# Four modulations move from TensorE's blocks in the attention stages to VectorE's sums in the feed-forward stages

## The chip, the cores and the metric

The kernel runs on one core of a Trainium2 chip. The metric is the device time of one execution in microseconds (us), as the median of several runs; before the change it is 1739.68 us (three runs, 1738.67 to 1740.33). A core has five engines with an instruction queue each: TensorE (PE, its weight loads shown apart as PEld), VectorE (DVE), ScalarE (ACT), GpSimd (POOL) and SyncE (SP, which here issues most DMAs).

## The reference

Two layers of a diffusion transformer's block over 256 tokens x and 256 context tokens, width 1024. A layer has a half feed-forward, an attention with three branches, and a second half feed-forward. Each of the three is normed, shifted, scaled and gated by modulations, nine a layer, each a product of a condition with a 1024 x 1024 piece of `w_ada`. There are two conditions (one for the tokens, one for the context).

```python
mod_x = (jax.nn.silu(c) @ w_ada[l] + b_ada[l]).reshape(bn, 1, N_MOD, d)
mod_c = (jax.nn.silu(c_ctx) @ w_ada[l] + b_ada[l]).reshape(1, 1, N_MOD, d)
h_x = _half_ffn(h_x, norm_g[l, 0], mod_x[:, :, 0], mod_x[:, :, 1], mod_x[:, :, 2], ffn1_up[l], ffn1_down[l])
a_x = _modulate(_rmsnorm(h_x, norm_g[l, 1]), mod_x[:, :, 3], mod_x[:, :, 4])
p_x = a_x @ w_in[l]
...
h_x = h_x + mod_x[:, :, 5] * (jnp.concatenate([o_a, o_b, o_c], axis=-1) @ w_out[l])
h_x = _half_ffn(h_x, norm_g[l, 2], mod_x[:, :, 6], mod_x[:, :, 7], mod_x[:, :, 8], ffn2_up[l], ffn2_down[l])
```

The context goes the same way, except that it ends with the second layer's attention. So modulations are numbered 0 to 17 over both layers (9 is the second layer's first); those from 14 on are needed for one condition only. The result is the normed h_x. All products are wanted in float32 precision.

## The kernel before

**Stages.** The program is one long sequence: feed-forward 1 of layer 0 (about 15 to 407 us of the trace), attention 0 (to about 612) with the w_out product behind it, feed-forward 2 of layer 0 (from about 640), feed-forward 1 of layer 1 (from about 1010), attention 1 (1377 to 1513) with its w_out product, feed-forward 2 of layer 1, and the final norm. Activations lie with features on partitions and tokens on the free axis; 512 tokens (both halves) go together where the context takes part, 256 where it does not.

**Dense products.** Each weight and each activation is kept as a high and a low part, and `mm3` (L344) makes three matmuls of one product: L348, L349 and L350. A stream of weight blocks is loaded by SP into three raw buffers of 1 MB (RAW_BUFS); `emit_split` (L291) makes from a piece of a block a slot of the pool `w`: ScalarE casts the high part (L306), VectorE subtracts for the low one (L309). The pool has 7 buffers (W_BUFS). `pump` splits ahead of need while the count of slots out, `st["out"]`, is below a limit `st["look"]` (6 in the feed-forward stages, less in the attentions); `take` (L331) hands out the next slot, and splits it on the spot if that was not done. `by_halves` (L532) is the start of a stage's products: it takes four slots and goes through one half of the tokens and then the other, as the normed operand comes from `apply` (ScalarE L437, VectorE L436 and L431), while the end of the stage before, `proj_out` (L466), still adds its last chunks to the residual (VectorE L461) and squares them (ScalarE L374).

**Modulations, two ways.** By TensorE: blocks of 128 rows by 2048 columns (two modulations, 1 MB) stand in the weight stream, between the attention's own blocks. `ada_quantum` (L175) multiplies one with four matmuls of 32 columns of weights and 512 moving columns (L181); eight blocks make a pair of modulations, which ScalarE copies out (L239) and TensorE turns into columns (L246). By VectorE: `ada_one` (L201) loads 128 rows by 512 columns (256 KB, L207) two blocks ahead and adds their multiple to an accumulator of the pool `w`, for each condition, with ScalarE for the first rows (L219) and VectorE for the others (L221). At the end of a modulation `ada_total` (L225) sums over the partitions with four matmuls against ones (L229), some time after the last block: 22 us by the emission clock, or 5 for an urgent one (2 or 8, where it is the first of its stage). Until then the accumulator counts as a slot out. Sixteen blocks make a modulation. `ada_step`, called once for each slot of a feed-forward stage, does ADA_RATE blocks, or 2 for an urgent modulation. Which modulation goes which way is set by MODS (by stage, VectorE) and ATT (by layer, pairs for TensorE).

**Order.** The order of each engine's instructions is that in which the Python code emits them. A clock of emitted TensorE work (`tick`) starts the deferred pieces (`later`). In an attention `run` (L928) goes through softmax units: scores (L838, L839) of one unit, work to fill in, then the transposes of the probabilities of the unit two before (`flip`: L878 for tokens, L883 for the context, copied out by ScalarE, L886). Products with v follow (`pv`: L912, its normalization's transposes L919, ScalarE L920 and L924). How many us of filling work stand in each gap is a table, FILL, and `piece` (L1048) picks it: the rest of w_in's products, products with v, the pooling (`pooled`: L1025, then ScalarE L1029 and VectorE L1030), then by turns a modulation block (`run_ada`) and two chunks' dense products with w_out's first half (`rest_out`, six matmuls for each chunk of two). What dense work is left after the last unit comes behind the last product with v.

Of the kernel before, what the change touches and what calls it, by code (L numbers as in the profile page):

```python
# [18 lines left out]
TX = 256  # L19
# [3 lines left out]
EPS = 1e-6  # L23
# [9 lines left out]
MODS = ((2, 3, 4, 5, 8), (9, 10, 11, 12), (13, 14, 15))  # L33
ATT = ([3], [8])
ADA_RATE = (1.3, 1.3, 1.3, 1)
# [15 lines left out]
def dit_kernel(  # L51
# [47 lines left out]
    pending = []  # L99
    clock = [0.0]  # L100
# [21 lines left out]
    stream = []  # L122
# [52 lines left out]
    def ada_quantum(g, k, raw):  # L175
        """128 rows of two of the modulations, by the tensor engine."""
        if k == 0:
            ada_ps[g] = ps_ada.tile([128, 512], F32, tag="ada", name="ada")
        ps = ada_ps[g]
        for j in range(4):  # L180
            PE.matmul(out=ps[32 * j:32 * j + 32, :], lhsT=sc[:, k, :], rhs=raw[:, j * 512:(j + 1) * 512], start=(k == 0), stop=(k == KD - 1))  # L181
        st["raws"] -= 1
        loads()
        if k == KD - 1:
            sb = ada_rows(ada_ps.pop(g))
            later(5.0, lambda: ada_columns(sb, [2 * g, 2 * g + 1], 2))
# [3 lines left out]
    def conds(m):  # L190
        """How many conditions a modulation is for: the context's tokens end with the second layer's attention."""
        return 1 if m >= 14 else 2
# [8 lines left out]
    def ada_one():  # L201
        """The next block of the modulations, 128 rows by 512 columns, that the vector engine does: it sums both conditions'
        multiples of the rows; the sums over partitions are the tensor engine's, once for a modulation."""
# [38 lines left out]
    def ada_columns(sb, ms, n):  # L242
        """Rows 32j (and the one after) of four groups of columns become columns of the modulations ms."""
# [27 lines left out]
    def next_main(force=False):  # L271
        """Whether the next weight block of the stream is on its way; ada blocks before it go to the tensor engine."""
# [7 lines left out]
    def run_ada():  # L280
        """Runs the next ada block of the stream, if that is what comes next."""
# [9 lines left out]
    def emit_split(between=None):  # L291
        """Splits the next slot of the stream into two float32r parts (ada blocks on the way go to the tensor engine)."""
# [51 lines left out]
    def mm3(ps, pairs, n, start, stop):  # L344
        """Accumulates products of split operands: pairs of ((wh, wl), (ah, al)); the first of each is stationary."""
# [17 lines left out]
    def acc_chunk(vs, k):  # L363
        """Squares of chunk k of the halves vs of the tokens; summed over chunks, but a half's last chunk apart."""
# [18 lines left out]
    def rsqrt(ps, n, scale):  # L383
        """1 / sqrt(ps * scale + EPS) of few elements, by Newton's steps from a guess at the exponent."""
# [27 lines left out]
    def spread(v, rb=None):  # L412
        """The tokens' factors on every partition."""
# [5 lines left out]
    def apply(v, i, a, pace=0.0, rb=None):  # L419
        """The operand of the next product: normed, scaled and shifted, in two parts."""  # L420
# [45 lines left out]
    def proj_out(src, kl, ppair, gate, both, final, after, each=None):  # L466
        """One part of a product into the residual. src(k) gives the moving operand; a slot has ppair chunks. In the final
        part the last two slots go by halves of the tokens, so that one half's norm runs under the other."""
# [35 lines left out]
    def boundary(i):  # L504
        """What follows a finished half: its statistic and its operand of the next product."""
# [26 lines left out]
    def by_halves(sl, a, both, evac):  # L532
        """Products of four slots, one half of the tokens after the other, chunk by chunk of the operand as it comes. Two
        products share a bank: the first start clears what the whole bank has had written."""
# [11 lines left out]
    def up_evac(pa, pb, g, m, nm, lo, hi):  # L546
        """g[m : m + nm] of the tokens lo:hi from the banks of both factors."""
# [89 lines left out]
    def attn_prep(l):  # L637
        """Bias of the neighbourhood's scores (masked), and the pooling weights as blocks of a diagonal."""
# [11 lines left out]
        # copies of a head's table at a pitch of 465, read back at a pitch of 464: row c starts c entries earlier  # L650
# [24 lines left out]
    def attention(l, a, both):  # L675
        """From the normed tokens to the operand of w_out and the first half of that product; both: the context's tokens
        are carried on too."""
# [20 lines left out]
        # k of the neighbourhood, k and v of the grouped heads: by halves of the tokens  # L698
        sl = [take() for _ in range(4)]

        def key_tile():
            """Keys of two heads: each one's high part on both halves of the rows, then both low parts; and some queries."""
# [12 lines left out]
        def split_queries(dst, src, scale=None):  # L715
            """Queries of two heads, each one's high part on its half of the rows and its low part on the other."""
# [10 lines left out]
        def rotate(q, n):  # L727
            """Rotary embedding of n chunks of the first TX tokens in place."""
# [15 lines left out]
        def k_post():  # L744
            """Norm and rotation of the grouped heads' keys."""
# [29 lines left out]
        # q and v of the neighbourhood  # L775
# [28 lines left out]
        # the pooling's matrices: each block of tokens on itself; on its neighbour they are in k_edge  # L804
# [9 lines left out]
        def queries(br, kind, hs):  # L814
            """Both heads' queries as they are multiplied."""
# [7 lines left out]
        def scores(br, kind, hs, t):  # L823
            """x: one block of 128 tokens over all keys; c: all of the context's tokens over its keys."""
# [42 lines left out]
        def flip(br, kind, hs, t, Ps):  # L867
            """Probabilities with the keys on partitions; the products with v once a pair of heads has them all."""
# [59 lines left out]
        def run(jobs, fill, before):  # L928
            """Units of softmax, each one's probabilities turned depth units later."""
# [19 lines left out]
        def stat_col(c, tb):  # L949
            """Where the statistics of chunk c's two heads lie, for a block of tokens."""  # L950
            return c // 2 * nb * 4 + tb * 4 + c % 2 * 2

        def q_post(j):
            """Rotation and norm of two chunks of queries."""
# [9 lines left out]
        def rest_in():  # L964
            """q of the grouped heads and u of the pooling."""
# [27 lines left out]
        def rest_out():  # L993
            """The product with w_out's first half: the neighbourhood's and the pooling's chunks."""
# [53 lines left out]
        def piece():  # L1048
            """A piece of the work that is independent of the units."""
# [21 lines left out]
        def before(n):  # L1071
            """What the unit n needs, beyond its queries."""
# [40 lines left out]
    with tc.manual_schedule():  # L1113
        # small operands, laid in rows and turned into columns
# [13 lines left out]
        def quarter_load(h, i, raw):  # L1128
            """Half of the rows of the first shift's and scale's chunks 2h and 2h + 1."""
# [19 lines left out]
        def load_pair(v, k2):  # L1149
            """Two chunks of half the tokens, turned."""  # L1150
# [7 lines left out]
        def quarter_ada(h):  # L1158
            """The products of two chunks of the shift and scale: each of the array's four groups of columns sums a quarter of
            the rows."""  # L1160
# [25 lines left out]
        # sums of squares of the tokens as they come, a token on a partition  # L1186
# [27 lines left out]
        def first():  # L1214
            """The first four slots' products, as the shift and scale and with them the operand's chunks come."""
# [45 lines left out]
        def last_chunk(ch):  # L1261
            """A chunk of the result, scaled by the last norm's gains."""
# [94 lines left out]
```

## Time and profile before

| | before |
|---|---|
| timed, median of 3 | 1739.68 us |
| profiled execution, span | 1741.7 us |
| dense products (L348, L349, L350), x7776 | 913.0 + 904.5 + 904.2 us of records that overlap |
| weight splits, casts L306 and subtractions L309, x312 each | 314.9 and 371.0 us |
| blocks of modulations by VectorE, L221, x308 | 216.0 us |
| blocks of modulations by TensorE, L181, 128 records (x64 matmuls) | 16.8 us by the sum of the groups of the instructions' table |
| totals L229, 96 records | 13.0 us |

The profiled execution's span lies 2.0 us above the timed median; sums are made against the span. A page row of an instruction group gives the line, the engine, the operation, what is written and read with the tile's partitions and elements, the count, the busy time, the mean length in ns, and the idle time of the engine just ahead with what ended most of it. A timeline row gives the start in us, the length, the engine, the line and the operation. Matmuls are pipelined, so the length of one is longer than the distance to the next; distances are taken from starts.

### The profile page before, as it was taken

Reading aid. Unit: us, or ns where it says so; the run is one execution under the profiler, and the core shown is the slowest. Engines: PE = TensorE matmul, PEld = TensorE weight load, DVE = VectorE, ACT = ScalarE, POOL = GpSimd, SP = SyncE. Lnnn points to the kernel's source line nnn. Section 1 sums busy time; section 2 is a strip of 40 time slices with the busy share of each in tenths; the row PEclk is TensorE's granted clock in tenths of the full one; section 3 lists DMA queues with packets and bytes.
Section 4 is the critical chain, followed back from the end, with each engine's and each line's share of the span. In section 5 each row is a group of like instructions: output and inputs, shape, how many; then the busy total and the mean of one; then the engine's idle time right before and its main releaser. Section 6 shows DMA issues by size and latency. Waiting matters only on the chain.

```text
span 1741.7 us, 23662 instructions
## 1 busy us (share of the span) xinstructions
PE 1706.1 (98%) x9512; PEld 1428.7 (82%) x9512; DVE 1025.0 (59%) x1748; ACT 664.8 (38%) x1087; POOL 33.3 (2%) x48
## 2 busy tenths in 40 slices
PE   6999999999999999999999999999999999989998
PEld 4778888889886688888888898888888987789998
DVE  5666676566545586666664466545433656565554
ACT  4431322324545644323333243223222356554443
POOL 0000200000000000000000000020000000000000
PEclk8999999999999999999999999999999999989999
DMA  9755555431304325544653335455533133546561
GB/s 316 207 175 168 155 179 173 151 121 49 109 25 160 107 73 168 164 140 140 192 152 122 92 88 183 150 160 174 146 97 97 49 110 146 169 133 205 164 201 50
DMA packets 295335, 246.48 MB, mean 142 GB/s; under 512 B 9377, under 2 KB 262442, under 8 KB 293176
## 3 DMA queue, kind: packets, MB, share of 16 engines
q1 hardware_dynamic: 292680, 241.30, 44.7%
q0 software_dynamic: 1088, 2.15, 0.5%
q8 instruction: 75, 1.23, 0.3%
q10 hardware_dynamic: 1456, 1.52, 0.3%
q14 instruction: 36, 0.29, 0.1%
HBM read 243.88 MB, written 2.00 MB: 141 GB/s over the span
## 4 chain that ended last, share of the span: by engine, by line
PE 90%; DVE 4%; DMA 2%; ACT 2%; issue 1%; SPq 0%; DVEq 0%; ACTq 0%
PE mm L348 27%; PE mm L350 27%; PE mm L349 27%; PE mm L839 2%; PE mm L912 1%; PE aux L878 1%; PE mm L838 1%; DVE w L309 1%; PE ada L181 1%; DMA ada_raw<-in_w_ada_dram 1%; DVE ada_acc L221 1%; PE ada L229 1%; DMA raw<-in_w_ada_dram 1%; ACT w L306 1%; PE aux L409 0%
## 5 line engine op out<-in xcount | busy, mean ns | idle before, releaser
L348 PE MATMUL mm<-act,w 128*128 128x512 f32 (+1 forms) x2592 | 913.0, 352 | 5.6 <-ACT act L437 3.3
L350 PE MATMUL mm<-act,w 128*128 128x512 f32 (+1 forms) x2592 | 904.2, 349 | 1.8 <-DVE w L309 1.8
L349 PE MATMUL mm<-act,w 128*128 128x512 f32 (+1 forms) x2592 | 904.5, 349 | 1.0 <-DVE act L431 0.9
L348 PEld LDWEIGHTS mm<-act,w 128*128 128x128 f32 x2592 | 494.1, 191 | 89.3 <-issue 19.4
L350 PEld LDWEIGHTS mm<-act,w 128*128 128x128 f32 x2592 | 494.0, 191 | 64.1 <-DVE w L309 2.4
L349 PEld LDWEIGHTS mm<-act,w 128*128 128x128 f32 x2592 | 494.3, 191 | 62.5 <-DVE act L431 1.7
L309 DVE TENSOR_TENSOR w<-raw,w 128x1024 fp32r<-128x1024 f32 (+1 forms) x312 | 371.0, 1198 | 245.6 <-ACT w L306 245.2
L306 ACT CAST w<-raw 128x1024 fp32r<-128x1024 f32 (+1 forms) x312 | 314.9, 1023 | 120.4 <-PE mm L350 93.6
L221 DVE SCALAR_TENSOR_TENSOR ada_acc<-ada_raw,sc,ada_acc 128x512 f32<-128x512 f32 x308 | 216.0, 746 | 47.9 <-DMA ada_raw<-in_w_ada_dram 24.7
L558 ACT CAST act<-gf 128x512 fp32r<-128x512 f32 (+1 forms) x87 | 49.7, 571 | 318.7 <-DVE gf L555 318.7
L461 DVE SCALAR_TENSOR_TENSOR hT<-mm,hgt,hT 128x256 f32<-128x256 f32 x168 | 75.1, 480 | 97.8 <-PE mm L350 97.6
L552 ACT ACTIVATE sil<-mm 128x512 f32<-128x512 f32 (+1 forms) x87 | 47.6, 547 | 214.8 <-PE mm L350 214.5
L555 DVE TENSOR_TENSOR gf<-sil,mm 128x512 f32<-128x512 f32 (+1 forms) x87 | 54.3, 625 | 94.0 <-PE mm L350 77.7
L559 DVE TENSOR_TENSOR act<-gf,act 128x512 fp32r<-128x512 f32 (+1 forms) x87 | 54.9, 631 | 55.5 <-ACT act L558 55.5
L374 ACT ACTIVATE sq<-hT 128x256 f32<-128x256 f32 (+1 forms) x52 | 25.5, 492 | 108.4 <-DVE hT L461 108.4
L437 ACT ACTIVATE act<-nt,modT 128x256 fp32r<-128x256 f32 x88 | 43.4, 507 | 49.3 <-DVE nt L436 49.2
L219 ACT ACTIVATE ada_acc<-ada_raw,sc 128x512 f32<-128x512 f32 x44 | 29.6, 718 | 47.4 <-DMA ada_raw<-in_w_ada_dram 36.7
L855 DVE TENSOR_REDUCE nm<-mm 128x1 f32<-128x512 f32 (+1 forms) x60 | 41.0, 686 | 7.9 <-PE mm L839 7.2
L863 ACT ACTIVATE P<-mm,nm,rq 128x512 f32<-128x512 f32 (+1 forms) x48 | 33.7, 707 | 22.3 <-DVE nm L860 21.0
L431 DVE SCALAR_TENSOR_TENSOR act<-nt,modT,act 128x256 fp32r<-128x256 f32 x88 | 41.3, 480 | 1.3 <-ACT act L437 1.3
L436 DVE SCALAR_TENSOR_TENSOR nt<-hT,gsc,aux 128x256 f32<-128x256 f32 x88 | 40.8, 476 | 1.8 <-PE aux L416 1.2
L886 ACT COPY PT<-aux 128x512 f32<-128x512 f32 x60 | 32.2, 588 | 16.9 <-PE aux L878 12.9
(154 smaller groups left out, 885.5 us busy)
## 6 DMA issues: line engine op xcount, KB each, us to landing
raw<-in_ffn_up_dram SPq DMA_DIRECT2D x172, 512.0 KB
ada_raw<-in_w_ada_dram SPq DMA_DIRECT2D x192, 256.0 KB
raw<-in_ffn_down_dram SPq DMA_DIRECT2D x32, 1024.0 KB
raw<-in_w_ada_dram SPq DMA_DIRECT2D x16, 1024.0 KB
raw<-in_ffn_down_dram SPq DMA_DIRECT2D x16, 768.0 KB
raw<-in_w_in_dram SPq DMA_DIRECT2D x10, 1024.0 KB
raw<-in_w_out_dram SPq DMA_DIRECT2D x8, 1024.0 KB
raw<-in_w_ada_dram SPq DMA_DIRECT2D x12, 512.0 KB
```

What stands on the lines that cost most here:

```text
L221: DVE.scalar_tensor_tensor(out=o, in0=raw, scalar=col, in1=o, op0=ALU.mult, op1=ALU.add)
L306: ACT.copy(out=wh, in_=sl)
L309: DVE.tensor_tensor(out=wl, in0=sl, in1=wh.bitcast(F32), op=ALU.subtract)
L348: PE.matmul(out=ps, lhsT=wh, rhs=ah, start=start and i == 0, stop=False)
L349: PE.matmul(out=ps, lhsT=wh, rhs=al, start=False, stop=False)
L350: PE.matmul(out=ps, lhsT=wl, rhs=ah, start=False, stop=stop and i == last)
L437: ACT.activation(out=acol(a, k, v * TX, v * TX + TX)[0], in_=t, func=AF.Identity, bias=modT[:, l * 72 + 3 * n * 8 + k, v:v + 1])
L461: DVE.scalar_tensor_tensor(out=hT[:, k, cols], in0=ps, scalar=gate[:, k, v:v + 1], in1=hT[:, k, cols], op0=ALU.mult, op1=ALU.add)
L552: ACT.activation(out=s[:, 0:n], in_=pa[:, 0:n], func=AF.Silu)
L555: DVE.tensor_tensor(out=u[:, 0:n], in0=s[:, 0:n], in1=pb[:, 0:n], op=ALU.mult)
L558: ACT.copy(out=gh, in_=uv)
L559: DVE.tensor_tensor(out=gl, in0=uv, in1=gh.bitcast(F32), op=ALU.subtract)
```

## The change

Three tables of numbers change; the rest of the diff deletes comments and docstrings. The pairs of modulations 6, 7 (`ATT` group 3) and 16, 17 (group 8) leave the weight stream, and join MODS: 6 and 7 in the first stage, 16 and 17 in the third. Modulation 8 moves from the first stage to the second. The rates of the first and third stage go from 1.3 to 1.5 blocks per slot. Blocks by stage were 80, 64 and 48; they are 96, 80 and 80.

```diff
-MODS = ((2, 3, 4, 5, 8), (9, 10, 11, 12), (13, 14, 15))
-ATT = ([3], [8])
-ADA_RATE = (1.3, 1.3, 1.3, 1)
+MODS = ((2, 3, 4, 5, 6, 7), (8, 9, 10, 11, 12), (13, 14, 15, 16, 17))
+ATT = ([], [])
+ADA_RATE = (1.5, 1.3, 1.5, 1)
```

The places where the order moves, as each engine has it:

ScalarE (ACT) at the end of the first feed-forward stage, where the first attention's products begin. `w_2915` is the fourth slot of w_in before the change. Before:

```order
L306 CAST w_2888<-raw_2717 128x1024
L239 COPY adasb_2913<-ada_2907 128x512
L306 CAST w_2915<-raw_2717 128x1024
L374 ACTIVATE sq_2931<-hT_84 128x256
L374 ACTIVATE sq_2960<-hT_84 128x256
L374 ACTIVATE sq_3014<-hT_84 128x256
L437 ACTIVATE act_3026<-nt_3030,modT_94 128x256
L437 ACTIVATE act_3026<-nt_3042,modT_94 128x256
L437 ACTIVATE act_3026<-nt_3053,modT_94 128x256
L374 ACTIVATE sq_3058<-hT_84 128x256
L437 ACTIVATE act_3026<-nt_3075,modT_94 128x256
```

In the changed kernel that slot is `w_3119`:

```order
L306 CAST w_2964<-raw_2771 128x1024
L374 ACTIVATE sq_2996<-hT_84 128x256
L374 ACTIVATE sq_3025<-hT_84 128x256
L374 ACTIVATE sq_3072<-hT_84 128x256
L437 ACTIVATE act_3084<-nt_3088,modT_94 128x256
L437 ACTIVATE act_3084<-nt_3100,modT_94 128x256
L437 ACTIVATE act_3084<-nt_3111,modT_94 128x256
L374 ACTIVATE sq_3116<-hT_84 128x256
L306 CAST w_3119<-raw_2771 128x1024
L437 ACTIVATE act_3084<-nt_3139,modT_94 128x256
```

The slot's cast has moved from ahead of the last squares and the first three chunks of the operand to behind them. Modulation 7's total, which gives its accumulator back, stands on TensorE some sixty matmuls into the first half's products, and the slot's first use ten matmuls in.

TensorE near the end of attention 0, from the context's third grouped unit on (L838, L839 scores; L883 transposes for the context; L912, L919 product with v). Before:

```order
L912 MATMUL mm<-PT,qkv 64x256 x16
L919 MATMUL aux<-ident,rec 128x128 x4
L348 MATMUL mm<-act,w 128x512
L349 MATMUL mm<-act,w 128x512
L350 MATMUL mm<-act,w 128x512
L348 MATMUL mm<-act,w 128x512
L349 MATMUL mm<-act,w 128x512
L350 MATMUL mm<-act,w 128x512
L883 MATMUL aux<-ident,P 128x128 x8
L838 MATMUL mm<-K,qst 128x256
```

Behind these come the scores of the last unit, twelve dense matmuls, L883 x24 and two products with v of eight. In the changed kernel the dense work is used up, and the last unit's scores end in this:

```order
L838 MATMUL mm<-K,qst 128x256
L839 MATMUL mm<-K,qst 128x256
L912 MATMUL mm<-PT,qkv 64x256 x16
L919 MATMUL aux<-ident,rec 128x128 x4
L883 MATMUL aux<-ident,P 128x128 x24
L912 MATMUL mm<-PT,qkv 64x256 x8
L919 MATMUL aux<-ident,rec 128x128 x4
```

The product with v has moved behind the last unit's scores, and no dense matmul stands between the last scores and the last transposes.

TensorE at the end of attention 1. Before, the last three transposes stand apart; the middle of it:

```order
L181 MATMUL ada<-raw,sc 32x512 x4
L878 MATMUL aux<-ident,P 128x128 x8
L348 MATMUL mm<-act,w 128x256
L349 MATMUL mm<-act,w 128x256
L350 MATMUL mm<-act,w 128x256
L348 MATMUL mm<-act,w 128x256
L349 MATMUL mm<-act,w 128x256
L350 MATMUL mm<-act,w 128x256
L181 MATMUL ada<-raw,sc 32x512 x4
```

In the changed kernel they are one row, behind twelve dense matmuls of which three are shown:

```order
L348 MATMUL mm<-act,w 128x256
L349 MATMUL mm<-act,w 128x256
L350 MATMUL mm<-act,w 128x256
L878 MATMUL aux<-ident,P 128x128 x24
L912 MATMUL mm<-PT,qkv 64x256 x16
L919 MATMUL aux<-ident,rec 128x128 x4
```

The blocks are gone, 18 of the 30 dense matmuls between the last scores and the last product with v have moved ahead of those scores, and the three flips follow one another.

## The prediction, on record before the result

> **What bounds the kernel now.** I read the page's busy shares first, then the chain that ended last, then a table of busy time by stage, then the waits.
>
> ```profile
> span 1741.7 us, 23662 instructions
> PE 1706.1 (98%) x9512; PEld 1428.7 (82%) x9512; DVE 1025.0 (59%) x1748; ACT 664.8 (38%) x1087; POOL 33.3 (2%) x48
> PE 90%; DVE 4%; DMA 2%; ACT 2%; issue 1%; SPq 0%; DVEq 0%; ACTq 0%
> ```
>
> TensorE is busy for 98% of the span and holds 90% of the chain, so the bound is the time that PE takes for its rows, and a PE row taken away is worth its own time unless a wait appears in its place. The stages differ. The next five rows are the first feed-forward stage, attention 0, the second and third feed-forward stages and attention 1 (stretch, then its length, busy PE, PEld, DVE, ACT, POOL, granted clock, DMA share, GB/s):
>
> ```profile
> 100.00:395.00 295.00, 294.65 (x1325) 238.96 (x1324) 188.90 (x263) 87.66 (x114) 9.82 (x16) 1.00 0.52 162
> 407.00:612.00 205.00, 203.09 (x1252) 154.72 (x1251) 112.20 (x274) 112.99 (x258) 6.37 (x5) 0.98 0.26 85
> 640.00:1000.00 360.00, 359.96 (x1710) 298.70 (x1711) 219.15 (x316) 114.06 (x152) 0.00 (x0) 1.00 0.45 141
> 1010.00:1368.00 358.00, 358.00 (x1706) 298.99 (x1706) 184.60 (x260) 106.90 (x142) 9.76 (x16) 1.00 0.44 135
> 1377.00:1513.00 136.00, 133.70 (x977) 108.00 (x978) 82.97 (x201) 77.73 (x163) 3.79 (x3) 0.97 0.37 127
> ```
>
> In the feed-forward stages PE has no gap, and VectorE stands idle for 36% (first), 39% and 48% of them. In the attentions PE idles 1.9 and 2.3 us in all, so hardly anything is hidden there either; what PE multiplies in them is on the path.
>
> **What is removed.** Sixteen blocks of four matmuls (L181; the trace has two records for each), eight in each attention, and a turn of columns (L246) for each eight. The chain has them, first and last of the 16:
>
> ```profile
> 534.90 1.00 PE ada L181 x8
> 1503.19 0.99 PE ada L181 x8
> 1490.05 1.06 PE L181 MATMUL ada<-raw,sc 128*32 128x512 f32 x8
> 1491.05 3.67 PE L912 MATMUL mm<-PT,qkv 128*64 128x256 f32 x32
> 1508.51 0.66 PE L246 MATMUL aux<-ident,adasb 128*128 128x128 f32 x4 [0.24 <-ACT PT L886]
> 1509.10 3.67 PE L912 MATMUL mm<-PT,qkv 128*64 128x256 f32 x32
> ```
>
> A block pushes what follows it back by 1.0 us, the columns by 0.6 us: 16 x 1.0 + 2 x 0.6 = **17.2 us** less. Their sixteen 1-MB loads become 64 loads of 256 KB on the same queue: equal bytes, beside a feed-forward DMA share of about 0.5, so I cost them at nothing.
>
> **What is added.** On PE, four totals (L229), in the feed-forward stages, with their columns:
>
> ```profile
> 393.97 1.06 PE L229 MATMUL ada<-ada_acc,ones 128*32 128x512 f32 x8
> 1252.91 0.64 PE L229 MATMUL ada<-ada_acc,ones 128*32 128x256 f32 x8
> ```
>
> Modulations 6 and 7 serve two conditions: 1.0 + 0.6 us each; 16 and 17 serve one: 0.6 + 0.3 us each (half the transposes). Together **+5.0 us**, all on the path, since PE has no gap there. On VectorE, 84 multiply-adds (L221), about 28 in each of the three stages:
>
> ```profile
> L221 DVE SCALAR_TENSOR_TENSOR ada_acc<-ada_raw,sc,ada_acc 128x512 f32<-128x512 f32 x308 | 216.0, 746 | 47.9 <-DMA ada_raw<-in_w_ada_dram 24.7
> DVE ada_acc L221 <- DMA ada_raw<-in_w_ada_dram: 24.7, 21, 3.3
> ```
>
> 216.0 / 308 = 0.70 us, so 20 us per stage, beside 106 us of VectorE's idle time in the first of those rows. I take nothing for it: weight slots are split three and more ahead, while a single wait for a block's DMA was at most 3.3 us. If that cover went, the price would be a 3.3 us wait of PE per stage, or 10 us (a rival below). The ScalarE starts (L219) have still more room.
>
> **Waits in place of what goes: the boundary.** In the first stage the sums now end later, so modulation 7's accumulator still holds a weight slot at the first boundary. The fourth w_in slot is split only when the products by halves ask for it. Before:
>
> ```profile
> 395.58 1.05 ACT L306 CAST w<-raw 128x1024 fp32r<-128x1024 f32 x1
> 396.67 1.22 DVE L309 TENSOR_TENSOR w<-raw,w 128x1024 fp32r<-128x1024 f32 x1
> 406.26 0.28 PE L348 MATMUL mm<-act,w 128*128 128x256 f32 x1
> 406.37 0.28 PE L349 MATMUL mm<-act,w 128*128 128x256 f32 x1
> 407.25 0.48 DVE L461 SCALAR_TENSOR_TENSOR hT<-mm,hgt,hT 128x256 f32<-128x256 f32 x1
> 407.77 0.42 ACT L374 ACTIVATE sq<-hT 128x256 f32<-128x256 f32 x1 [0.28 <-DVE hT L461]
> ```
>
> The split was ready 8 us early. In the new order its cast stands behind that L374 on ScalarE, and its subtract behind that L461 on VectorE: cast 408.2 to 409.2, subtract to 410.5. PE starts these products at about 406.26, one every 0.12 us, and wants the slot at the tenth, 407.3. It waits to 409.2, does two matmuls, waits to 410.5: **+2.9 us**. Behind it on PE stand all the first attention's products, so nothing gives it back. Bounds: 0, if the total came early enough to free the slot, and 3.2 (both operations from 407.3 on).
>
> **Waits in the attentions.** The L181 blocks also covered softmax and operand work. In attention 0's middle:
>
> ```profile
> 537.88 0.84 ACT L721 CAST qst<-qkv 64x256 fp32r<-64x256 f32 x2
> 539.37 1.13 PE L1025 MATMUL mm<-y,pwbd 128*128 128x256 f32 x4
> 541.67 0.46 ACT L1029 ACTIVATE act<-mm,colsB 128x256 fp32r<-128x256 f32 x1
> 543.19 0.48 DVE L1030 SCALAR_TENSOR_TENSOR act<-mm,colsB,act 128x256 fp32r<-128x256 f32 x1 [0.54 <-ACT act L1029]
> ```
>
> With the blocks gone the second scores reach the query split about 0.5 us before it is done, and dense products, now right behind the pooling's L1025, need its operand, which takes 2.0 us (541.67 to 543.67); six matmuls without it cover about 1 us, so 1.0 us is lost. Then the tail. Dense products that were spaced out by blocks are used up earlier, and the last transposes (L883 x24) follow a product with v instead of 12 dense matmuls:
>
> ```profile
> 594.56 0.37 ACT L920 COPY rec<-aux 128x256 f32<-128x256 f32 x1 [1.91 <-PE aux L919]
> 596.98 1.06 ACT L886 COPY PT<-aux 128x512 f32<-128x512 f32 x2
> 602.10 1.03 PE L883 MATMUL aux<-ident,P 128*128 128x128 f32 x8
> 603.37 1.14 PE L883 MATMUL aux<-ident,P 128*128 128x128 f32 x8 [0.24 <-ACT PT L886]
> 605.83 1.95 PE L912 MATMUL mm<-PT,qkv 128*64 128x256 f32 x16
> ```
>
> Three flips behind dense work took 605.83 - 602.10 = 3.7 us, paced by ScalarE's copies. After a product with v ScalarE first has 596.98 - 594.56 = 2.4 us of other work, of which flips with two banks in hand cover about 1: +1.5 us. Attention 0 loses 0.5 + 1.0 + 1.5 = **3.0 us** of its gain. In attention 1 the final three flips come together too (before, dense work stood between them) and the columns' cover is gone: **+1.5 us**. Bounds for the two together: 0 and 9, about half of what was removed.
>
> Sum so far: -17.2 + 5.0 + 2.9 + 3.0 + 1.5 = **-4.8 us**: 1741.7 to 1736.9 in the profiled execution. That execution lies 2.0 us above the timed median of 1739.7, which becomes 1734.9.
>
> **The clock.** The attentions have stretches at a granted clock of 0.50:
>
> ```profile
> 496.30:499.70 3.40, 3.40 (x19) 2.37 (x17) 0.84 (x2) 1.77 (x4) 0.00 (x0) 1.00 0.80 267
> 499.70:506.50 6.80, 6.80 (x29) 6.44 (x29) 3.20 (x8) 1.93 (x8) 3.02 (x2) 0.50 0.05 20
> 602.10:605.50 3.40, 2.92 (x23) 2.31 (x22) 0.88 (x2) 2.46 (x5) 0.00 (x0) 1.00 0.01 2
> 1404.20:1411.00 6.80, 6.44 (x28) 5.91 (x28) 5.90 (x9) 3.80 (x5) 1.18 (x1) 0.50 0.58 162
> ```
>
> At half clock 3.4 us of PE work costs 1.7 us more, so a stretch of 6.8 us costs 3.4. The change leaves three places bare: the boundary (2.9 us idle within about 3.2), attention 0's tail (flips thinner than at 602) and attention 1's tail. I give them chances of 0.5, 0.65 and 0.45 to bring a drop, 1.6 drops at about 1.7 us in the mean; one or two, +2.6 us, are likeliest: **1737.5 us**.
>
> Here a rule speaks. The row before the drop at 499.70 shows PE busy for all of its 3.40 us, with few columns in it. The Trainium skill, TensorE: Matmul & The Clock Gate, section "HAM oscillation — how this bites in real kernels", says instead that what has to be avoided is a PE idle gap of more than about 3.4 us. By that rule none of the three places drops, and the time would be that of the first rival; the row at 499.70 does not bear the rule out as it stands, but the row at 602.10, thin and without a drop, shows that thin stretches can go by.
>
> **The rivals.**
> - No new drop (or as many old ones go as new ones come, since the phase of all later work shifts): 1734.9. For it: the row at 602.10. Against: the row at 499.70. Chance 0.24.
> - The covers suffice: the slot frees in time and other work hides the flips. Then -17.2 + 5.0 = -12.2, **1727.5**. Against: ScalarE's order at the boundary and the 0.24 us waits that the flips have already. Chance 0.08.
> - Slower by the clock: all three places drop for two windows each, as at 499.70: 3 x 3.4 = 10.2 on 1734.9, **1745**. It decides when the bare stretch spills into the next window, which the boundary's split 2.9 us or the tails' thin flips can do. Chance 0.13.
> - Slower by VectorE: prefetched slots run out and PE waits for L309 once per feed-forward stage, 10 us: **1747.5**. Against: 36% idle VectorE. Chance 0.07.
> - The forecast, one or two drops, 1735 to 1742: chance 0.48.
>
> **How the numbers follow.** 0.2%, about what timing tells from no change, is 3.5 us: faster means under 1736.2, slower over 1743.2. Faster takes the second rival, most of the first and the forecast's low edge: 0.32. Slower takes both slow rivals and a little of the forecast: 0.22. The rest, 0.46, is the same. The range, 1731.5 to 1745.5, reaches from half of the covers sufficing to the clock rival, and leaves out the rest.
>
> **What would show it.** L181 gone, L221 at 392; no PE gap in the feed-forward stages; at the boundary a PE wait on w from L306 and then L309, together near 2.9 us (nothing there, and that step was wrong); the gaps before the flips, named after PT copies; granted clock of 0.50 behind these places. Attention 0 should shorten by about 5 us after its first products, attention 1 by about 7. A feed-forward stage that grows by over 3.5 us, or waits on L309 there, would prove me wrong, as would a time under 1731.

## The result, and the profile after

The changed kernel takes 1758.4 us (median of 4 runs, 1755.15 to 1760.78), against 1740.0 for the kernel before in the same measurement: a ratio of 1.0108, 95% interval 1.0092 to 1.0123. It is 18 us slower, where 1737.5 was forecast and 1745.5 was the range's upper end.

The page of the changed kernel, busy shares and the chain by engine:

```profile
span 1759.0 us, 23637 instructions
PE 1709.2 (97%) x9420; PEld 1436.7 (82%) x9420; DVE 1079.7 (61%) x1832; ACT 672.8 (38%) x1101; POOL 33.8 (2%) x48
PE 84%; DVE 6%; DMA 3%; ACT 3%; issue 2%; SPq 0%; DVEq 0%; ACTq 0%
L221 DVE SCALAR_TENSOR_TENSOR ada_acc<-ada_raw,sc,ada_acc 128x512 f32<-128x512 f32 x392 | 275.1, 746 | 74.5 <-DMA ada_raw<-in_w_ada_dram 50.4
```

The work moved as meant (L221 at 392, no L181 left), but PE's busy time did not fall: 12 us less of work shows as 3 us more, since part of it ran at half clock, and PE's share of the chain is six points of the span lower. The waits of TensorE, summed by what was waited for; the rows that are new or longer than before:

```profile
PE aux L409 <- DVE acc L380: 7.6, 4, 3.5
PE aux L883 <- ACT PT L886: 4.4, 1, 4.4
PE ada L229 <- DVE ada_acc L221: 3.3, 2, 2.2
PE mm L350 <- DVE w L309: 2.5, 3, 1.1
PE aux L878 <- ACT PT L886: 2.4, 4, 0.9
PE mm L348 <- ACT w L306: 1.7, 1, 1.7
```

The columns are the us in total, how often, the longest. The L229 row holds two places: 2.2 us at modulation 8's total in the second feed-forward, and 1.1 us at 109 us in the first, where the kernel before already waits 0.4. To see where the loss arises, I compare the start of the same dense matmul (the n-th of both traces) and take the difference:

| place | before, us | after, us | later by |
|---|---|---|---|
| end of the first feed-forward | 400.34 | 401.86 | 1.5 |
| after the first boundary | 427.81 | 442.26 | 14.5 |
| end of attention 0 | 610.78 | 624.02 | 13.2 |
| end of the second feed-forward | 1003.44 | 1021.56 | 18.1 |
| end of the third feed-forward | 1348.38 | 1368.72 | 20.3 |
| behind attention 1 | 1540.94 | 1558.66 | 17.7 |

So +12.9 at the boundary, -1.2 in attention 0 (-5.6 had been forecast), +4.9 in the second feed-forward (+1.6), +2.2 in the third (+1.8), -2.6 in attention 1 and its w_out (-7.1). Of the 12.9, 1.6 are modulation 7's own total with its columns, which TensorE now runs at 433 us, behind the boundary.

**The boundary.** Before, the statistic (L409) of the first half waits for nothing:

```profile
400.82 0.50 PE L409 MATMUL aux<-ones,acc 128*128 128x1 f32 x4
```

Timeline of VectorE, TensorE and ScalarE there, in the changed kernel:

```profile
389.49 2.73 DVE L221 SCALAR_TENSOR_TENSOR ada_acc<-ada_raw,sc,ada_acc 128x512 f32<-128x512 f32 x4
...
396.39 1.41 DVE L221 SCALAR_TENSOR_TENSOR ada_acc<-ada_raw,sc,ada_acc 128x512 f32<-128x512 f32 x2
...
402.03 1.41 DVE L221 SCALAR_TENSOR_TENSOR ada_acc<-ada_raw,sc,ada_acc 128x512 f32<-128x512 f32 x2
403.35 0.68 DVE L380 TENSOR_TENSOR acc<-acc,sq 128x512 f32<-128x512 f32 x1
403.95 0.48 DVE L461 SCALAR_TENSOR_TENSOR hT<-mm,hgt,hT 128x256 f32<-128x256 f32 x1
404.92 0.43 DVE L380 TENSOR_TENSOR acc<-acc,sq 128x256 f32<-128x256 f32 x1 [0.48 <-ACT sq L374]
...
405.40 1.01 PE L409 MATMUL aux<-ones,acc 128*128 128x1 f32 x4 [2.89 <-DVE acc L380]
...
415.20 1.03 ACT L306 CAST w<-raw 128x1024 fp32r<-128x1024 f32 x1
416.26 1.23 DVE L309 TENSOR_TENSOR w<-raw,w 128x1024 fp32r<-128x1024 f32 x1 [1.42 <-ACT w L306]
416.28 0.39 PE L348 MATMUL mm<-act,w 128*128 128x256 f32 x1 [1.66 <-ACT w L306]
...
417.54 0.39 PE L350 MATMUL mm<-act,w 128*128 128x256 f32 x1 [0.76 <-DVE w L309]
```

Two waits. The late slot is as forecast: 2.9 us, the cast behind a square and then the subtract. The other was not: eight multiply-adds of the last modulation, 5.5 us of VectorE, stand among its last operations of the stage, the last two at 402.03, and all of them ahead of the sum of squares (L380 at 404.92) that the first half's statistic (L409) needs. TensorE starts that at 405.40 and has idled 2.9 us for it; with the start of the statistic itself the dense work behind it comes 3.5 us later than in the old order. And each wait is followed by a half clock. A window here is a stretch of the trace, mostly of 3.4 us, since the stretches at 0.50 in these traces last 3.4, 6.8, 10.2 or 13.7 us (apart from the last one, which the program's end cuts off). The table of windows at the two waits, one line ahead of each drop and the drop:

```profile
401.40:404.80 3.40, 1.10 (x10) 0.90 (x8) 3.03 (x5) 0.33 (x1) 0.00 (x0) 1.00 0.01 4
404.80:411.70 6.90, 6.30 (x29) 6.30 (x30) 3.16 (x14) 0.92 (x3) 0.00 (x0) 0.51 0.00 0
415.10:418.50 3.40, 1.46 (x11) 1.26 (x11) 2.01 (x3) 1.63 (x3) 0.00 (x0) 1.00 0.00 0
418.50:425.30 6.80, 6.80 (x34) 6.80 (x34) 5.49 (x21) 2.32 (x5) 0.00 (x0) 0.50 0.58 158
```

The same table, at the two other new drops, in attention 0's tail and attention 1's middle:

```profile
609.60:613.00 3.40, 0.66 (x4) 0.42 (x4) 2.83 (x10) 1.56 (x7) 0.00 (x0) 1.00 0.00 0
613.00:619.90 6.90, 5.21 (x24) 3.89 (x26) 1.28 (x7) 4.47 (x11) 0.00 (x0) 0.51 0.00 1
1483.40:1486.90 3.50, 2.53 (x12) 1.33 (x11) 2.02 (x5) 2.30 (x7) 0.00 (x0) 0.99 0.00 0
1486.90:1493.70 6.80, 6.18 (x19) 3.48 (x20) 3.97 (x12) 4.74 (x12) 0.00 (x0) 0.50 0.01 4
```

Four new stretches of 6.8 us at half clock, which cost up to 3.4 us each. At the last one PE was busy for 2.53 of 3.5 us ahead of the drop, with scores and transposes. Over the timed runs the mean granted clock fell from 0.990 to 0.982. A span times its clock is what it would be if every half-clock stretch had been full work: 1721 us before, 1725 after. So some 4 of the 18 us are waits net of the work saved, and up to 14 are the clock's.

**Attention 0's tail and the total of modulation 8.** The last transposes waited 4.4 us:

```profile
607.61 0.66 PE L919 MATMUL aux<-ident,rec 128*128 128x128 f32 x4
608.49 0.42 DVE L921 TENSOR_TENSOR rec<-mm,rec 128x256 f32<-128x256 f32 x1 [5.55 <-ACT rec L920]
610.95 0.68 DVE L855 TENSOR_REDUCE nm<-mm 128x2 f32<-128x512 f32 x1
614.69 3.82 PE L883 MATMUL aux<-ident,P 128*128 128x128 f32 x16 [4.36 <-ACT PT L886]
```

The last unit's scores were done at 604. Its maximum (L855) ran only at 610.95: the clock's step inside `scores` had released a product with v before the softmax was emitted, so on VectorE the normalization of that product (L921, waiting 5.6 us for ScalarE's copy L920, which itself comes behind TensorE's L912 and L919) stood ahead of the maximum. In the second feed-forward, modulation 8's total, urgent now and due 5 us after its last block, came before VectorE had done the last blocks. The profile names 2.2 us of wait; by the starts, 728.44 for the next dense matmul against 724.23 for the total, it took 4.2 us, where a total that does not wait takes 1.0 (723.37 to 724.37 in total8, below):

```profile
724.23 1.05 PE L229 MATMUL ada<-ada_acc,ones 128*32 128x512 f32 x4
724.66 2.74 DVE L221 SCALAR_TENSOR_TENSOR ada_acc<-ada_raw,sc,ada_acc 128x512 f32<-128x512 f32 x4
727.46 1.05 PE L229 MATMUL ada<-ada_acc,ones 128*32 128x512 f32 x4 [2.18 <-DVE ada_acc L221]
```

### The profile page after: what moved, and what is told of

Read it like the earlier page. It is cut to its first block, busy times and chain, and to the rows that moved or that the text cites. A ratio compares the mean times of both kernels' runs of the same rounds, so it can differ in the third digit from the quotient of the medians.

```text
span 1759.0 us, 23637 instructions
## 1 busy us (share of the span) xinstructions
PE 1709.2 (97%) x9420; PEld 1436.7 (82%) x9420; DVE 1079.7 (61%) x1832; ACT 672.8 (38%) x1101; POOL 33.8 (2%) x48
## 4 chain that ended last, share of the span: by engine, by line
PE 84%; DVE 6%; DMA 3%; ACT 3%; issue 2%; SPq 0%; DVEq 0%; ACTq 0%
PE mm L348 25%; PE mm L349 25%; PE mm L350 25%; DMA ada_raw<-in_w_ada_dram 2%; DVE ada_acc L221 2%; DVE w L309 2%; PE mm L912 2%; PE mm L839 1%; PE aux L878 1%; ACT w L306 1%; PE mm L838 1%; PE ada L229 1%; DVE hT L461 1%; DVE acc L380 1%; PE aux L409 1%
## 5 line engine op out<-in xcount | busy, mean ns | idle before, releaser
L348 PEld LDWEIGHTS mm<-act,w 128*128 128x128 f32 x2592 | 496.3, 191 | 88.9 <-issue 17.7
L221 DVE SCALAR_TENSOR_TENSOR ada_acc<-ada_raw,sc,ada_acc 128x512 f32<-128x512 f32 x392 | 275.1, 746 | 74.5 <-DMA ada_raw<-in_w_ada_dram 50.4
L219 ACT ACTIVATE ada_acc<-ada_raw,sc 128x512 f32<-128x512 f32 x56 | 37.9, 717 | 62.8 <-DMA ada_raw<-in_w_ada_dram 55.2
L855 DVE TENSOR_REDUCE nm<-mm 128x1 f32<-128x512 f32 (+1 forms) x60 | 41.0, 686 | 5.1 <-PE mm L839 4.4
L863 ACT ACTIVATE P<-mm,nm,rq 128x512 f32<-128x512 f32 (+1 forms) x48 | 33.7, 707 | 23.9 <-DVE nm L860 22.6
L886 ACT COPY PT<-aux 128x512 f32<-128x512 f32 x60 | 32.6, 590 | 13.7 <-PE aux L878 9.2
```

The costliest lines, as they stand in the source:

```text
L221: DVE.scalar_tensor_tensor(out=o, in0=raw, scalar=col, in1=o, op0=ALU.mult, op1=ALU.add)
L348: PE.matmul(out=ps, lhsT=wh, rhs=ah, start=start and i == 0, stop=False)
```

## The experiments

Theory S: the loss sits at places in the order (where the sums end, what stands ahead of the last softmax, when the urgent total comes) and the drops of the clock follow the idle or thin stretches there. Rival V: VectorE, its queue or its transfers are overloaded by the 84 added multiply-adds. All medians stand against the kernel before in the same measurement, 1739.4 to 1740.3 us. "Full" is the mean of span times clock over the timed runs (before: 1720 to 1721).

| run | median us | ratio, 95% interval | mean clock | full, us |
|---|---|---|---|---|
| changed kernel | 1758.4 | 1.0108 (1.0092 to 1.0123) | 0.982 | 1725 |
| rate18 | 1746.1 | 1.0043 (1.0028 to 1.0058) | 0.986 | 1720 |
| slot7 | 1754.2 | 1.0079 (1.0060 to 1.0097) | 0.983 | 1722 |
| soft_first | 1752.4 | 1.0070 (1.0044 to 1.0096) | 0.985 | 1724 |
| total8 | 1754.3 | 1.0092 (1.0077 to 1.0107) | 0.982 | 1721 |
| three | 1742.4 | 1.0017 (1.0007 to 1.0027) | 0.986 | 1717 |
| only_first | 1752.1 | 1.0076 (1.0054 to 1.0097) | 0.987 | 1728 |
| only_second | 1739.2 | 0.9999 (0.9989 to 1.0010) | 0.988 | 1717 |
| dummy4 | 1741.8 | 1.0018 (1.0004 to 1.0033) | 0.989 | 1721 |
| dummy2 | 1741.0 | 1.0011 (0.9999 to 1.0023) | 0.990 | 1721 |
| dummy2b | 1738.0 | 0.9990 (0.9982 to 0.9999) | 0.990 | 1718 |
| covered | 1739.8 | 1.0002 (0.9990 to 1.0014) | 0.987 | 1716 |
| covered_first | 1737.8 | 0.9987 (0.9977 to 0.9998) | 0.990 | 1718 |

The changed kernel, slot7, soft_first, total8 and only_first have four timed executions each, and the intervals of the other four reach into that of the changed kernel. Every execution of soft_first and of only_first (1749.8 to 1754.4) is faster than each of the changed kernel's (from 1755.2 on); slot7 and total8 overlap with it, so there the argument rests on the traces.

**rate18: the sums end earlier.**

```diff
-ADA_RATE = (1.5, 1.3, 1.5, 1)
+ADA_RATE = (1.8, 1.3, 1.5, 1)
```

> The changed kernel with one number different: the first stage's rate of VectorE blocks 1.8 per slot instead of 1.5, so that modulation 7's blocks and its total end before the first attention's products begin. Theory S (where the sums end decides): the statistic's wait of about 3 us, the slot's wait of 2.9 us and the two clock drops at the first boundary go, so 10 to 12 us faster than the changed kernel, about 1747. Rival V (the 84 added multiply-adds load VectorE, its queue or the DMA): a higher rate loads them more, so 1758 or slower.

12.3 us faster than the changed kernel. The boundary costs nothing: the difference to the kernel before is 1.8 us ahead of it and 1.6 behind it. VectorE at the place of the first timeline, and the statistic:

```profile
398.91 0.68 DVE L380 TENSOR_TENSOR acc<-acc,sq 128x512 f32<-128x512 f32 x1
400.47 0.42 DVE L380 TENSOR_TENSOR acc<-acc,sq 128x256 f32<-128x256 f32 x1 [0.48 <-ACT sq L374]
...
402.61 0.50 PE L409 MATMUL aux<-ones,acc 128*128 128x1 f32 x4
```

L380 no longer stands behind an L221, and L409 waits for nothing. VectorE does the same sums at a higher rate and the time falls, so V, as an overload, is wrong for this loss; what counts is which sums are left at the stage's end.

**slot7: the slot's wait alone.**

```diff
-            st["out"] += 1
+            st["out"] += int(m != 7)
...
-        st["out"] -= 1
+        st["out"] -= int(m != 7)
```

> The changed kernel, with modulation 7's accumulator left out of the count of slots out, so that the fourth w_in slot is split ahead again; TensorE's order is the same, the sums still run up to the stage's end. Theory S: of the 12.9 us at the first boundary the slot's wait (2.9 us) and the second drop of the clock (about 2.5 us) go and the statistic's wait (2.9 us) and the first drop stay, 4 to 6 us faster than the changed kernel, 1753. Rival (what counts is one late VectorE, and the slot's wait only takes the place of another): under 2 us.

4.2 us faster than the changed kernel. The second drop is gone with the slot's wait, the first one stays with the statistic's:

```profile
399.00:403.00 4.00, 1.39 (x12) 1.19 (x10) 3.52 (x6) 0.42 (x1) 0.00 (x0) 1.00 0.42 118
403.00:410.00 7.00, 6.72 (x32) 6.73 (x33) 3.31 (x15) 0.83 (x2) 0.00 (x0) 0.51 0.32 82
410.00:424.00 14.00, 13.96 (x118) 13.77 (x117) 12.83 (x40) 6.84 (x15) 0.00 (x0) 1.00 0.01 2
```

So the boundary's two waits have each their own drop; both drops stand there in the profiles of soft_first, total8 and only_first too, which have both waits, and neither in those of rate18, three and covered, which have none.

**soft_first: the last softmax ahead of the product with v.**

```diff
-            tick(0.9)
-            return [soft(br, kind, h, t, S[i]) for i, h in enumerate(hs)]
+            Ps = [soft(br, kind, h, t, S[i]) for i, h in enumerate(hs)]
+            return [Ps, tick(0.9)][0]
```

> The changed kernel with the softmax of a unit emitted ahead of the clock's step behind its scores; TensorE's order is the same, and VectorE and ScalarE have a unit's maximum and exponentials ahead of a product with v that the clock releases there (one place in each attention with grouped heads, and two in which rotations or the pooling's operand stood ahead). Theory S: the 4.4 us wait of the last transposes in the first attention and the clock drop behind it go, 4 to 7 us faster than the changed kernel, 1751 to 1754. Rival: the last unit's softmax takes that long in any order, so less than 1 us.

6.0 us faster, with TensorE's order unchanged. The last maxima run at once, and the last transposes start at 609.78 in place of waiting 4.4 us (those are timeline rows of this run):

```profile
602.14 0.69 DVE L855 TENSOR_REDUCE nm<-mm 128x2 f32<-128x512 f32 x1 [0.56 <-PE mm L839]
602.95 0.68 DVE L855 TENSOR_REDUCE nm<-mm 128x2 f32<-128x512 f32 x1
607.15 0.42 DVE L921 TENSOR_TENSOR rec<-mm,rec 128x256 f32<-128x256 f32 x1 [3.32 <-ACT rec L920]
609.78 1.14 PE L883 MATMUL aux<-ident,P 128*128 128x128 f32 x8 [0.79 <-ACT PT L886]
```

What is left in the flips, 0.24 + 0.51 + 0.79 + 0.24 us, is 1.8 us, or 1.3 more than the 0.5 of before; the prediction had 1.5 there. The drop at the tail is gone in this profile. The edit has a price that was not expected: in attention 0's middle, two more exponentials (L863) stand on ScalarE ahead of the pooling's operand (L1029), and the dense matmuls wait for it. The changed kernel and rate18 have no such wait, while soft_first, three, covered and covered_first have it:

```profile
PE mm L348 <- ACT act L1029: 1.7, 1, 1.7
```

**total8: modulation 8's total later.**

```diff
-            later(5.0 if m == st["urgent"] else ADA_TOT[st["ffn"]], lambda: ada_total(m, acc))
+            later((9.0 if m == 8 else 5.0) if m == st["urgent"] else ADA_TOT[st["ffn"]], lambda: ada_total(m, acc))
```

> The changed kernel with modulation 8's total (urgent) 9 us of the emission clock behind its last block instead of 5, which puts it 21 matmuls later in the second feed-forward. Theory S: TensorE's wait for the last multiply-adds there, 3.3 us, goes, and the columns still come before the first residual needs them, so 3 us faster than the changed kernel, 1755. Rival V (VectorE is behind by more than one total): the wait moves along or appears at the residual, less than 1 us.

The wait at this total is gone from the trace, the second feed-forward costs about 1.6 us more than before instead of 4.9, and the median is 4.1 us below the changed kernel's, though its interval (1.0077 to 1.0107) touches that of the changed kernel.

```profile
723.37 1.06 PE L229 MATMUL ada<-ada_acc,ones 128*32 128x512 f32 x8
```

**three: all three corrections.**

> The changed kernel with the three corrections together: rate 1.8 in the first stage, softmax ahead of the clock's step, modulation 8's total at 9. Theory S: the three places are apart, so the gains add, 12 + 6 + 3 = 21 us off 1758, 1737, a little faster than the kernel before. Rival: part of the gains is one and the same clock drop or is given back at a later place, 1742 or more.

1742.4: 16 us off, not 21, and 0.17% over the kernel before, which is the rival's number. The waits at the three places went as expected, and at full clock the kernel is 4 us ahead of the one before. That lies near the 4.8 of the prediction's sum without the clock, but in part by luck: the sum holds 2.9 us for the slot at the boundary, which does not wait here, and nothing of the 1.7 us behind the softmax's new place. The clock has taken that back and more: 0.986 against 0.990 is 7 us. Its profile has these two stretches:

```profile
596.40:599.80 3.40, 1.86 (x14) 1.24 (x12) 2.06 (x7) 2.36 (x6) 0.00 (x0) 1.00 0.00 0
599.80:603.20 3.40, 3.40 (x17) 2.46 (x17) 1.07 (x6) 2.10 (x5) 0.00 (x0) 0.50 0.00 0
1463.40:1466.80 3.40, 2.42 (x11) 1.15 (x10) 1.72 (x4) 2.22 (x6) 0.00 (x0) 1.00 0.00 0
1466.80:1477.00 10.20, 9.68 (x35) 5.51 (x35) 4.26 (x12) 5.15 (x13) 0.00 (x0) 0.50 0.01 2
```

**only_second and only_first: the change's halves.** Modulations 16 and 17 alone (ATT ([3], []), the first two stages as before), and all but 16 and 17 (ATT ([], [8])).

> The second half of the change alone: 16 and 17 on VectorE in the third stage at a rate of 1.5, everything before the third stage as before the change. Theory S: even, 1738 to 1742. Rival V: a third of the loss, about 1746. Rival C (the prediction's sum without a new clock drop): 5 us faster, 1735.

> The changed kernel with modulations 16 and 17 back as TensorE blocks in the second attention, and the third stage as before the change. Theory S: the whole loss lies in the first boundary, the first attention's tail and modulation 8's total; the second half of the change is about even (2 us lost in the third stage, about 2 won in the attention), so 1756 to 1760. Rival V: a third of the added VectorE work is gone, so about 6 us faster, 1752.

Alone, the second half is even, as S had it, but not for S's reason: 4 us of work are saved at full clock, and the clock (0.988 against 0.990) takes them. The other run missed S's number: without 16 and 17 the changed kernel is 6 us faster, not the same, by the clock (0.987 against 0.982) and not by work (1728 against 1725). Its 1752 is also V's number, so this run alone does not tell S from V; rate18 and slot7 do. Why the second half's drops cost more behind a late first half is not shown; in the table of windows the drops of single executions fall on differing places.

**dummy4, dummy2, dummy2b: filling the thin middle of attention 1.** On only_second; the added matmuls multiply a table that is no longer used, and nobody reads the result.

```diff
-                        if not run_ada():
+                        if run_ada():
+                            pass
+                        elif l and next(dummies, 0):
+                            dps = ps_ada.tile([128, 512], F32, tag="ada", name="ada")
+                            for j in range(4):
+                                PE.matmul(out=dps[32 * j:32 * j + 32, :], lhsT=sc[:, 0, :], rhs=bm[:, 0:512], start=True, stop=True)
+                            tick(0.93)
+                        else:
                             return False
```

> The second half of the change alone (16 and 17), with four matmul groups whose product nobody reads at the four places in the second attention's middle where the TensorE blocks of 16 and 17 stood (4 matmuls of 512 columns each, 4.0 us in all). Theory C (the blocks kept the granted clock up): the drop that the second half alone has there (0.50 for 6.8 us from 1466) goes, and with it 3.4 us and about 1 us of waits, so the 4.0 us cost nothing, within 1.5 us of the second half alone, 1738 to 1741. Rival (the drop costs little, or comes from elsewhere): 4 us slower than it, 1743.

> As the run with four groups, with two of them only, one behind the other ahead of the transposes at which TensorE waits for ScalarE's copies (1.9 us of work). Theory C: they fill the thin window, the drop goes, and the waits cover part of them, so 1 to 3 us faster than the second half alone, 1736 to 1738. Rival: 1 to 2 us slower than it, 1741.

> The second half of the change alone with two matmul groups that nobody reads behind the pooling's unit in the second attention's middle (1.9 us of work in the thin stretch), without the other change that the earlier run of this kind made to the first attention's emission. Theory C: the drop there goes in most executions, and 1 to 2 us of its 3.4 are left over, 1737 to 1739. Rival: they only add their time, 1741.

The first two missed theory C's numbers by 1 and 3 us: the granted clock came up (0.989 and 0.990), but the edit of these two also took hold in attention 0: beside one tile for all groups and a step of the emission clock at each call, it leaves out the second `run_ada()`, by which a gap takes a modulation block when no dense work may be taken. TensorE's order there is another one, and about 2 us were lost at the tail, so they are not a clean test. With the edit shown here (dummy2b) the median is 1738.0. The ratio, 0.9990 against 0.9999 for only_second, puts it 1.5 us below that, with 1.9 us of matmuls more; the intervals overlap, so the gain in time is not certain, but the windows show the clock plainly. The same place in the kernel before, in only_second and in dummy2b:

```profile
1462.90:1466.30 3.40, 3.40 (x27) 1.59 (x19) 1.61 (x4) 2.38 (x6) 0.00 (x0) 1.00 0.69 237
1466.30:1473.10 6.80, 6.80 (x46) 3.81 (x45) 4.42 (x12) 5.07 (x13) 0.00 (x0) 1.00 0.99 401
```

```profile
1462.90:1466.30 3.40, 2.42 (x12) 1.37 (x11) 1.85 (x5) 2.20 (x7) 0.00 (x0) 1.00 0.01 4
1466.30:1473.10 6.80, 6.29 (x21) 3.42 (x21) 4.14 (x12) 4.91 (x12) 0.00 (x0) 0.50 0.00 1
```

```profile
1462.90:1466.30 3.40, 3.31 (x21) 0.94 (x21) 2.02 (x5) 2.33 (x6) 0.00 (x0) 1.00 0.00 1
1466.30:1473.10 6.80, 5.62 (x39) 3.52 (x37) 3.85 (x11) 4.64 (x11) 0.00 (x0) 1.00 0.00 1
```

Useless matmuls in the window before keep the clock at 1.00, even though PE then idles more in the 6.8 us behind (5.62 busy, 6.29 before). One profile of each would leave chance as a rival, since drops move; but over all the kernels the place is consistent. The eight profiles without blocks or added matmuls in attention 1's middle (the changed kernel, rate18, slot7, soft_first, total8, three, only_second, covered) all have a drop of 6.8 or 10.2 us there, and the six with one or the other (before, only_first, covered_first, dummy4, dummy2, dummy2b) have none. So the L181 blocks that were removed here had a use besides their result.

**covered and covered_first: the dense work stays where it was.** On three, with a floor, for each unit, on how many of the 16 pieces of six dense matmuls must be left.

```diff
+FLOOR = ({10: 13, 11: 12, 12: 10, 13: 9, 14: 7, 15: 4, 16: 2}, {9: 6, 10: 5, 11: 4, 12: 2})
...
-                    if missing[0] or next(gen, "end") == "end":
+                    if missing[0] or floor[1] <= floor[0] or one() == "end":
```

> The run with three corrections, and with it a floor on how much of the dense work each gap among the softmax units may use, so that the dense matmuls stand in both attentions' second halves as before the change, without the TensorE blocks between them. Theory K (the blocks were worth their time as work that keeps the granted clock up, and the dense matmuls at the tail too): the drop at 600 goes, the thin middle of the second attention stays, 2 to 3 us faster than the three corrections, 1739 to 1740. Theory W (waits decide, not the clock): the flips' waits are covered, 1 us faster, 1741; and if the whole of the removed time came through, 1736.

> As the run with floors, with 16 and 17 left to TensorE blocks in the second attention as before the change. Theory K: the second attention has no new drop at its middle, which took back what 16 and 17 won, so the same as the run with floors within 2 us, and 1737 to 1740; the first attention's blocks still cost it one drop at its thin middle or tail, so no more than 2 us faster than before. Theory W: 16 and 17 give about 3 us, so the run with floors is 3 us faster than this one.

covered lies 2.6 us below three, level with the kernel before: the lowest time at full clock of all (1716), at a clock of 0.987. Its profile has no drop at 600 any more, and still one at attention 1's middle (10.2 us from 1468.5). But it has two others of 3.4 us in attention 0, at 441.1 and at 550.3, the second right behind the 1.7 us wait for the pooling's operand. covered_first, which leaves 16 and 17 to TensorE (and has one at 545.5 in that same place), has the clock of before (0.990) and is the fastest, 0.9987 (0.9977 to 0.9998), or 2.3 us by that ratio. This is K's order, not W's, though K had it at no more than 2 us below the kernel before, and the intervals of the two runs overlap, so the order is likely and not certain. It takes half of the TensorE blocks away and beats that kernel by an amount at the edge of what can be measured.

## Why the prediction was wrong, point by point

- **The work (-17.2 + 5.0): right for what was added, near for what was removed.** In the third feed-forward +1.8 was forecast for the totals and 2.2 came; the second feed-forward costs 1.6 more, as forecast, once modulation 8's total does not wait (total8). What was removed has no run that shows it alone: at full clock the version with the three corrections lies about 4 us under the kernel before, where the sum without the boundary's 2.9 is -7.7.
- **"I take nothing for it" (VectorE's 20 us per stage): this step failed.** On the average of a stage the cover was there, no weight slot was late within one. At the two places where TensorE needs VectorE's newest result it was not: the statistic behind the stage's last sums (3.5 us), and an urgent total 5 us behind its blocks (3.2 us by the starts). The prediction had looked at what waits for a slot, and not at what else stands in VectorE's queue.
- **The slot at the boundary (+2.9): right**, 2.9 us, by its mechanism.
- **The tail of attention 0 (+1.5): incomplete.** The flips' waits were about right (1.3 us in soft_first), but the row order was read on TensorE alone. On VectorE the softmax of the last unit had moved behind a product with v: 4.4 us more.
- **The other waits in the attentions (0.5 + 1.0 and 1.5): sizes and places wrong, by little.** The changed kernel's trace has no wait in attention 0's middle. In attention 1 the flips waited 2.4 us, over half of it in the middle (0.85 and 0.52), where no wait had been named.
- **The clock (+2.6): mechanism right, size wrong, and by the most.** Three bare places with one window of 1.7 us for about half of them were assumed; there were four drops of 6.8 us, so up to 13.6 us. The boundary brought two instead of one, the third came at the tail that was named, the fourth in attention 1's middle, which was not. The rule that the prediction weighed (the Trainium skill, TensorE: Matmul & The Clock Gate, section "HAM oscillation — how this bites in real kernels": no idle gap of PE over about 3.4 us) does not decide here. At attention 0's tail the idle gap was 4.4 us, and there rule and trace agree, though the clock fell 2.7 us into it; the boundary's gaps were 2.9, 1.7 and 0.8 us and those in attention 1's middle under 1 us, and the drops came all the same, behind windows with 1.10 to 2.53 us of busy PE.
- **The rivals.** "Slower by the clock" (1745) had the mechanism for the larger part; "slower by VectorE" (1747.5) had the engine but the wrong place. They were taken to exclude each other; the waits at the boundary and at attention 0's tail each brought a drop with them, so they came together. The wait at modulation 8's total brought none in the changed kernel's profile, and the drop in attention 1's middle came without VectorE.

## What to carry to other kernels

A wait at a stage's edge is paid twice where it leaves TensorE's window thin: once as the wait and once as half clock after it. Work that TensorE does between softmax units keeps the clock up, so ask, before taking it away, what else fills that stretch; where nothing does, the saving may not arrive. And when work goes to an engine with 40% idle time, look not at the average but at the few instructions there that another engine waits for, and at what stands ahead of each of them in the new order.

## What the runs showed of the hardware

A drop to half clock needs no window without work on TensorE: 2.42 us busy of 3.40, with scores and transposes, was followed by 6.8 us at 0.50, and the same stretch with 3.31 us busy was not. Its place is not fixed: the drop at 499.7 that the kernel before shows is missing at that spot in the profiled execution of only_second, which has the same instructions up to there. The spread of single executions goes with the clock: of the 25 of the kernel before that were timed beside three, the fastest (1735.7 us) had a mean granted clock of 0.993 and the slowest (1745.9) 0.985, and span times clock spreads over 6 us where the span spreads over 10.

Busy PE alone does not tell which window is thin: the prediction's row at 496.30 has PE busy for all of its 3.40 us, and a drop follows. The moving columns of the matmul records tell more. A stretch of 3.4 us of dense products has 7,680 of them. In the 14 profiles, between 50 and 1700 us, the 3.4 us ahead of each of the 71 drops had at most 2,832. Few columns did not suffice, though: eleven stretches at full clock that were as thin (1,408 to 2,822) were not followed by a drop. Some records can be missing from a trace, so these counts are lower bounds.
